# The first mixer's output projection as seven half-size block products, with weight operands prepared beside the recurrence

## The chip, the cores and the metric

The kernel runs on one core of a Trainium2 chip. Five engines work side by side and are ordered by semaphores: TensorE (PE: matmuls, with weight loads shown as PEld), VectorE (DVE), ScalarE (ACT), GpSimd (POOL) and SyncE (SP, which here only issues DMAs). Each engine takes its instructions in the order in which they were written for it. The metric is the device time of one execution in microseconds. Three runs of the kernel before gave 2483.78, 2484.63 and 2484.67 us, a median of 2484.63 us.

## The reference

A trunk of two layers on a 1024 x 1024 activation (1024 tokens, 1024 features), all in float32. The part that the change touches is the first layer's mixer: two branches of 512 features, a spatial gate (`a_out`) and a gated delta rule, a recurrence over the tokens (`b_out`). Both are joined and projected back to 1024 features, and the result is added to the residual `h`, which then goes through a norm into the MLP:

```python
hn = rms_norm(h, ln_mix_e[i])
proj = hn @ w_in_e[i]
a_out = gmlp_spatial_gate(jax.nn.gelu(a_uv), gmlp_v_gain[i], gmlp_ws[i], gmlp_bs[i])
b_out = gated_deltanet(b_qkv, b_z, b_beta, b_a, gdn_conv[i], gdn_a_log[i],
                       gdn_dt_bias[i], gdn_out_gain[i])
h = h + jnp.concatenate([a_out, b_out], axis=-1) @ w_out_e[i]
# every layer goes on with
hn = rms_norm(h, ln_mlp[layer])
h = h + jnp.square(jax.nn.relu(hn @ w_mlp1[layer])) @ w_mlp2[layer]
```

The second layer's mixer is a differential attention, and each layer ends with a gated per-layer embedding. They are not touched.

## The kernel before

**Layout and precision.** The activation is held transposed, features on the 128 partitions: eight feature tiles k or m, and for each two halves of 512 tokens (0 and 1). A matmul takes a 128 x 128 weight block and a 128 x 512 operand. Each float32 operand is split into a rounded part hi and a remainder lo (`split`: a cast on ACT, L315, and a subtraction on DVE, L319), and a product is three matmuls, hi·hi, hi·lo and lo·hi (`mm3`). All matmuls are issued through a helper at L82, so one line number stands for nearly all of them; the tiles' names tell them apart.

**Stages around the change.** `even_mix` runs the first mixer. Its generator `fill` yields after every few matmuls: the input projections (384 steps) and then `mixing()`. The recurrence (`prep` and `step` for chunks 0 to 7) takes its own instructions at a high priority, and between its pieces `pump` takes a number of steps from `fill`; `FILLS` says how many beside each chunk. `Ordered` keeps a filler matmul from being issued more than `LAG` slots ahead of the recurrence. The order of each engine's instructions is made when the program is built, by priority and a simulated time: what is written later can be issued earlier if its inputs and its buffer are free. Tiles of one tag share that tag's slots, so a tile waits for a slot until all who used a former one are done.

**The output projection.** `mixing()` runs `mix_out(0, ...)`, the product for token half 0, as filler. For each output tile m, the weight columns are loaded from `w_out` (into tag raw, 8 slots), split into tag w (12 slots), and multiplied by the eight operand tiles `mixed[0][k]`; the sum goes into the residual tile `acc` (loaded from `h_dram`, added at L1654), whose square is added up for the norm (`add_square`), and the tile is stored to `h_dram` (L1656). `second_gates` is woven in: it makes the gate branch of half 1. After the loop over chunks `put_b(1)` transposes the recurrence's output for half 1, `put_ab` splits it (L1998 and L1999), and `mix_out(1, ...)` runs in `trunk`. Its start issues the norm of half 0: `rms` sums the squares on TensorE, takes the power on POOL (L360), writes the 512 factors to DRAM and reads them back as rows of all partitions (L364, L366, `far=True`), and `norm` scales (L1669), casts (L1675) and subtracts (L1676) each of the eight tiles. `mix_out(1)` also takes five steps of `prepare`, which prepares weights of the second layer from POOL's queue. Then `mlp` begins, first with products of half 0 (`front`), whose weights go through raw and w.

**Seven products elsewhere.** `mlp`, `ple` and `values` already compute 2 x 2 block products with seven half-size products instead of eight (Strassen-Winograd). `prepare_gate` and `ple` do it with weight operands that are summed and split ahead, put into `gate_dram`, and loaded ready.

**Names and lines.** `FILLS`, `prepare_gate` (L249), `split` (L315, L319), `rms` (L349 to L366), `mix_out` (L1613), `put_ab` (L1995), `put_b` (L2002), `mixing` (L2300), `pump` (L2327), the tags raw, w, B, t (four slots), sqs0 and sqs1, and the PSUM tags mm, tr, aux, sc (two banks each).

## Time and profile before

| | us |
|---|---|
| three runs, median | 2484.63 |
| the profiled execution | 2483.4 |
| its span on the core | 2481.7 |
| PE busy | 2468.6 |
| DVE busy | 1856.5 |
| ACT busy | 1352.8 |
| POOL busy | 334.6 |

The profiled execution is one of its own, 1.2 us below the median of the three runs; its span is 1.7 us below its time. A busy engine is one that has an instruction under way; matmuls overlap in a pipeline, so the duration of one is longer than the distance to the next. Rows of groups show busy time and the mean duration in ns, then the idle time before them and what ended it. Rows of DMAs show how many transfers of what size there were and the median us from issue to landing. The recurrence runs from about 206 to 364 us, the output projection from 364 to 463 us, and the first MLP matmul starts at 462.99 us.

### The profile page before, as it was taken

How to read it: one execution, taken by the hardware profiler on the slowest of the kernel's cores; microseconds unless marked ns; L12 is line 12 of the kernel's file. 1: busy time of each engine (PE TensorE's matmuls, PEld its weight loads, DVE VectorE, ACT ScalarE, POOL GpSimd, SP SyncE). 2: the span in 40 equal slices, each digit the busy share in tenths (PEclk: the TensorE clock that was granted, in tenths of full speed). 3: DMA queues.
4: the chain of work that ended last, by engine and by line, in shares of the span. 5: the costliest groups of instructions: out<-in, count | busy, mean ns of one | idle time of the engine just before them, and what ended most of it. 6: DMA issues, size and time to landing. Idle time of an engine off the chain costs nothing.

```text
span 2481.7 us, 39487 instructions
## 1 busy us (share of the span) xinstructions
PE 2468.6 (99%) x13417; PEld 2100.4 (85%) x13417; DVE 1856.5 (75%) x3598; ACT 1352.8 (55%) x2752; POOL 334.6 (13%) x419
## 2 busy tenths in 40 slices
PE   9999999999999999999999999999999999999999
PEld 8898998887888888888889999988788888888887
DVE  7868665788877878777858777776878657788586
ACT  6635473565556445644527777764655554445452
POOL 0211221101111202411112232310000000000000
PEclk9999999999999999999999999999999999999999
DMA  8464435659778957985461311476467458666651
GB/s 240 127 188 108 141 118 186 216 191 320 275 263 312 331 184 239 329 263 189 155 204 52 100 66 58 138 235 210 140 219 249 168 172 307 187 197 196 196 175 64
DMA packets 330131, 478.17 MB, mean 193 GB/s; under 512 B 50276, under 2 KB 161864, under 8 KB 329928
## 3 DMA queue, kind: packets, MB, share of 16 engines
q1 hardware_dynamic: 314136, 426.87, 53.0%
q0 software_dynamic: 15232, 48.25, 5.6%
q8 instruction: 105, 1.72, 0.3%
q14 instruction: 98, 0.80, 0.1%
q10 hardware_dynamic: 560, 0.53, 0.1%
HBM read 327.67 MB, written 147.86 MB: 192 GB/s over the span
## 4 chain that ended last, share of the span: by engine, by line
PE 84%; issue 6%; DMA 4%; DVE 4%; ACT 1%; POOL 1%; SPq 0%; DVEq 0%; POOLq 0%; ACTq 0%
PE mm L82 72%; PE po L82 3%; PE qk L82 2%; PE tr L85 2%; PE aux L82 2%; DMA qk_dram<-w 1%; DVE w L319 1%; DMA gate_dram<-w 1%; DVE g L393 0%; DVE lg L1422 0%; DMA rd<-r 0%; DMA raw<-in_w_mlp_dram 0%; DMA t<-in_p_dram 0%; DMA graw<-gd 0%; ACT w L315 0%
## 5 line engine op out<-in xcount | busy, mean ns | idle before, releaser
L82 PE MATMUL mm<-g,w 128*128 128x512 f32 x2592 | 601.9, 394 | 0.0
L82 PEld LDWEIGHTS mm<-g,w 128*128 128x128 f32 x2592 | 486.7, 188 | 114.1
L315 ACT CAST w<-raw 128x512 fp32r<-128x512 f32 x550 | 335.3, 617 | 405.0 <-PE mm L82 273.3
L82 PE MATMUL mm<-hi,w 128*128 128x512 f32 x1696 | 545.1, 396 | 1.4 <-DVE w L319 1.3
L319 DVE TENSOR_TENSOR w<-raw,w 128x512 fp32r<-128x512 f32 x550 | 372.9, 686 | 173.8 <-ACT w L315 146.1
L82 PE MATMUL mm<-w,hi 128*128 128x256 f32 (+2 forms) x2112 | 438.1, 302 | 0.6 <-DVE k L1332 0.6
L82 PEld LDWEIGHTS mm<-hi,w 128*128 128x128 f32 x1696 | 317.9, 188 | 75.7 <-DVE w L319 2.1
L82 PEld LDWEIGHTS mm<-w,hi 128*128 128x128 f32 x2112 | 338.5, 188 | 17.1 <-DVE k L1332 1.3
L82 PE MATMUL mm<-lo,w 128*128 128x512 f32 x848 | 334.4, 395 | 0.5 <-DVE lo L1676 0.5
L82 PE MATMUL mm<-w,lo 128*128 128x256 f32 (+2 forms) x1056 | 316.0, 300 | 0.0
L82 PE MATMUL mm<-t,w 128*128 128x512 f32 x1152 | 271.3, 394 | 0.5 <-DVE g L393 0.5
L82 PEld LDWEIGHTS mm<-t,w 128*128 128x128 f32 x1152 | 216.4, 188 | 50.9 <-issue 0.9
L82 PEld LDWEIGHTS mm<-w,lo 128*128 128x128 f32 x1056 | 198.8, 188 | 7.9
L82 PEld LDWEIGHTS mm<-lo,w 128*128 128x128 f32 x848 | 159.5, 188 | 35.9 <-DVE lo L1676 1.0
L319 DVE TENSOR_TENSOR g<-graw,g 128x512 fp32r<-128x512 f32 x216 | 147.0, 683 | 4.4 <-DMA gd<-g 1.6
L315 ACT CAST g<-graw 128x512 fp32r<-128x512 f32 x216 | 132.8, 617 | 22.7 <-DMA graw<-gd 10.9
L1425 ACT ACTIVATE lg<-lg,nm 128x128 f32<-128x128 f32 (+7 forms) x128 | 99.3, 776 | 38.6 <-DVE nm L1422 37.5
L360 POOL TENSOR_TENSOR r<-ms,mhalf 128x4 f32<-128x4 f32 x12 | 17.1, 1427 | 739.1 <-DVE ms L358 707.9
L462 ACT ACTIVATE g<-g 128x512 f32<-128x512 f32 x100 | 63.0, 631 | 69.2 <-DVE g L393 69.1
L1422 DVE CUSTOM_DVE_ANT_0 lg<-qk,al 128x512 f32<-128x512 f32 (+3 forms) x128 | 74.2, 586 | 20.3 <-PE qk L82 17.8
L82 PE MATMUL mm<-ohi,w 128*128 128x512 f32 x256 | 83.6, 399 | 0.3 <-DVE acc L1654 0.3
L82 PE MATMUL mm<-ahi,w 128*128 128x512 f32 x256 | 83.1, 400 | 0.3 <-ACT ahi L1998 0.2
(397 smaller groups left out, 3836.4 us busy)
## 6 DMA issues: line engine op xcount, KB each, us to landing
raw<-in_w_mlp_dram SPq DMA_DIRECT2D x352, 256.0 KB, 3.7
graw<-gd SPq DMA_DIRECT2D x224, 256.0 KB, 3.3
gd<-g SPq DMA_DIRECT2D x192, 256.0 KB, 3.6
acc<-h_dram SPq DMA_DIRECT2D x64, 256.0 KB, 4.6
qk_dram<-w POOLq DMA_DIRECT2D x64, 256.0 KB, 5.2
keep<-in_w_mlp_dram SPq DMA_DIRECT2D x64, 256.0 KB, 5.0
w<-qk_dram SPq DMA_DIRECT2D x64, 256.0 KB, 4.2
raw<-in_w_in_e_dram SPq DMA_DIRECT2D x60, 256.0 KB, 3.8
```

Source lines behind the costliest of these rows:

```text
L82: self._next(self.engine.matmul(*a, **k))
L85: self._next(self.engine.transpose(*a, **k))
L315: inst = self.nc.scalar.copy(hi, src)
L319: inst = (lo_engine or self.nc.vector).tensor_tensor(lo, src, f32(hi), ALU.subtract)
L360: nc.gpsimd.tensor_tensor(r, ms, self.mhalf[:, 0:4], ALU.pow)
L462: nc.scalar.activation(g, src, AF.Relu)
L1422: nc.vector.tensor_tensor_reduce(out=lg[:, k0:k1], in0=ps[:, : k1 - k0], in1=al[:, u0 + k0 : u0 + k1], scale=-0.5 ** (hd + 1), scalar=3.0e ...
L1425: nc.scalar.activation(lg[:, :n], lg[:, :n], AF.Exp, bias=nm[:, r, nch - 1 : nch], scale=-1.0, accum_out=me.sums[:, b, r : r + 1])
```

## The change

The weight `w_out` is seen as 2 x 2 blocks of 512 x 512, the operand `mixed` as 2 x 2 blocks (feature half by token half). `prepare_mix` forms, for each of four row tiles k, the seven left operands (four sums or differences and three plain blocks), splits them and stores hi and lo in `mix_dram`; its loads and stores are issued by POOL, the stores of one operand at the start of the next (`late`). Its 29 steps are taken by `pump` on every fourth filler step after step 260. All 28 operands go through one slot, B, of hi and lo; x and y live in the slots sqs0 and sqs1, z in the ring t.

`put_ab` now also forms the right operands: half 0's tiles are stored in `halves`; t1 = half 0 minus half 1 of the gate's features, t2 = half 0 of the recurrence's features minus t1 (also stored), t4 = half 1 of those minus t2. t3, the difference of the two feature halves of token half 0, is formed at the start of `mix_seven`. Half 0 of the gate's features is no longer split itself.

`mix_seven` replaces both `mix_out` calls of the first layer. It runs the products 3, 1, 5, 6, 7 as filler (80 steps), then, after `put_b(1)`, 2 and 4 (32 steps). Each product loads 16 of the 56 x 2 prepared tiles, half of them into tag w, half into tag raw; hi and lo are used straight from there. Four PSUM banks `x` (two of mm, two of tr) hold product 1 and collect 6, 7 and 4 on top of it; the other products go through mm, aux and sc. `add` puts a product into the residual tiles, and with `done` adds the squares and stores. After product 7 half 0 is complete; the norm of half 0 is started inside product 2 and its scaling is written into product 4. Five steps of `prepare` are taken, two before product 4 and three after it. `put_b(1)` gets the high priority. `FILLS` goes from 20, 20, 20, 20, 26, 26, 28, 28 to 18, 18, 18, 18, 24, 26, 30, 30.

```diff
+BEFORE = 260
-FILLS = (20, 20, 20, 20, 26, 26, 28, 28)
+FILLS = (18, 18, 18, 18, 24, 26, 30, 30)
+    def prepare_mix(self, w):
+        nc = self.nc
+        self.mix_dram = self.dp.tile([7, 4, 2, P, HT], F32, name="mix_dram")
+        late = []
+        def put(n, k, src):
+            for out, t in late:
+                nc.gpsimd.dma_start(out, t)
+            late.clear()
+            both = self.slot("B", [P, 2, HT], F32R, "wm")
+            for j, t in enumerate(self.split(src, both[:, 0], both[:, 1])):
+                late.append((self.mix_dram[n - 1, k, j], f32(t)))
+        def get(t, j, l, k):
+            nc.gpsimd.dma_start(t, w[(4 * j + k) * P : (4 * j + k + 1) * P, l * HT : (l + 1) * HT])
+        def tt(out, a, b, op=ALU.subtract):
+            nc.vector.tensor_tensor(out, a, b, op)
+        def pair(k):
+            x, y = (self.sp.tile([P, HT], F32, tag=f"sqs{i}", name=self.nm("wm"), bufs=1) for i in range(2))
+            get(x, 1, 1, k)
+            get(y, 0, 1, k)
+            return x, y
+        x, y = pair(0)
+        yield
+        for k in range(4):
+            put(4, k, x)
+            tt(y, y, x, ALU.add)
+            yield
+            z = self.tmp()
+            get(z, 0, 0, k)
+            put(5, k, y)
+            yield
+            put(1, k, z)
+            tt(y, y, z)
+            yield
+            put(6, k, y)
+            tt(x, x, y)
+            yield
+            put(7, k, x)
+            get(x, 1, 0, k)
+            yield
+            put(2, k, x)
+            tt(x, x, y)
+            yield
+            put(3, k, x)
+            if k < 3:
+                x, y = pair(k + 1)
+            yield
+        for out, t in late:
+            nc.gpsimd.dma_start(out, t)
...
+    def mix_seven(self, h_dram, gain_next, gates, halves, t1s, t2s, side):
+        rings = ("w", WB), ("w", WB), ("raw", RB), ("raw", RB)
...
+        def load(n):
+            a = []
+            for k in R:
+                tag, bufs = rings[k]
+                a.append([self.wp.tile([P, 1, HT], F32R, tag=tag, name=self.nm("w"), bufs=bufs)[:, 0] for _ in range(2)])
+                for j, t in enumerate(a[k]):
+                    nc.sync.dma_start(f32(t), self.mix_dram[n - 1, k, j])
+            return a
...
+        def add(m, h, ps, done=False):
+            t = acc(m, h)
+            nc.vector.tensor_tensor(t, t, ps, ALU.add)
+            if done:
+                self.add_square(h, t)
+                nc.sync.dma_start(h_dram[m, :, h * HT : (h + 1) * HT], t)
+        def third():
+            a[3] = load(3)
+            for q in R:
+                if q == 1:
+                    a[1] = load(1)
+                y = bank("mm")
+                yield from product(q, a[3], self.mixed[0][4:], y, True)
+                add(q, 0, y)
+            a[5] = load(5)
...
+        x = [bank(t) for t in ("mm", "tr", "mm", "tr")]
+        for q in R:
+            yield from product(q, a[1], self.mixed[1][0:4], x[q], True)
+            add(q, 1, x[q])
+        a[6] = load(6)
+        for q in R:
+            y = bank("aux")
+            yield from product(q, a[5], t1s, y, True)
+            add(q, 0, y)
+            add(4 + q, 0, y)
+        a[7] = load(7)
+        for q in R:
+            yield from product(q, a[6], t2s, x[q])
+            add(q, 0, x[q], True)
+        a[2] = load(2)
+        for q in R:
+            yield from product(q, a[7], t3s, x[q])
+            add(4 + q, 0, x[q], True)
+        a[4] = load(4)
+        yield True
+        for q in R:
+            y = bank("sc")
+            yield from product(q, a[2], self.mixed[1][4:], y, True)
+            if q == 0:
+                self.rb[0] = self.rms(0, self.sqs[0], far=True)[1]
+            add(q, 1, y, True)
+        next(side, None)
+        next(side, None)
+        for q in R:
+            yield from product(q, a[4], t4s, x[q])
+            if q == 0:
...
+                    inst = nc.vector.scalar_tensor_tensor(t, t, gain_next[:, m : m + 1], self.rb[0], ALU.mult, ALU.mult)
...
+            add(4 + q, 1, x[q], True)
+        for _ in range(3):
+            next(side, None)
...
         def put_ab(hf, k, pt):
...
+            if not hf:
+                t = self.tmp()
+                nc.scalar.copy(t, flat(pt))
+                nc.sync.dma_start(halves[k], t)
+            if hf or k > 3:
+                self.mixed[hf][k] = self.split(flat(pt), *self.hs_parts(hf, k))
+            if hf and k < 4:
+                u, v = self.tmp(), self.tmp()
+                nc.sync.dma_start(u, halves[k])
+                nc.vector.tensor_tensor(u, u, flat(pt), ALU.subtract)
+                t1s.append(self.split(u, *self.hs_parts(1, 4 + k)))
+                nc.sync.dma_start(v, halves[4 + k])
+                nc.vector.tensor_tensor(v, v, u, ALU.subtract)
+                t2s.append(self.split(v, *self.hs_parts(0, 4 + k)))
+                nc.sync.dma_start(t2_dram[k], v)
+            elif hf:
+                u = self.tmp()
+                nc.sync.dma_start(u, t2_dram[k - 4])
+                nc.vector.tensor_tensor(u, flat(pt), u, ALU.subtract)
+                self.t4s.append(self.split(u, *self.hs_parts(1, k - 4)))
...
         def mixing():
+            for _ in parts:
+                pass
             self.new_hs()
+            seven.append(self.mix_seven(h_dram, gain_next, second_gates(), halves, t1s, t2s, side))
+            yield from iter(lambda: next(seven[0]), True)
...
+                if done > BEFORE and done % 4 == 0:
+                    next(parts, None)
...
-        for _ in put_b(1):
+        with self.tc.high_priority(EARLY):
+            for _ in put_b(1):
+                pass
+        for _ in seven[0]:
             pass
```

77 lines of the change are left out of this document (55 added, 22 removed).

## The prediction

> **What bounds the kernel now.** I read the page's busy shares and its chain of waits first, then the busy time of the stages around the change, then the pitch of the matmuls inside the chain.
>
> ```profile
> PE 2468.6 (99%) x13417; PEld 2100.4 (85%) x13417; DVE 1856.5 (75%) x3598; ACT 1352.8 (55%) x2752; POOL 334.6 (13%) x419
> PE 84%; issue 6%; DMA 4%; DVE 4%; ACT 1%; POOL 1%; SPq 0%; DVEq 0%; POOLq 0%; ACTq 0%
> 206.00:364.00 158.00, 158.00 (x1277) 151.19 (x1275) 105.74 (x246) 85.60 (x235) 38.19 (x31) 1.00 0.40 118
> 364.00:463.00 99.00, 98.74 (x468) 80.56 (x468) 65.02 (x122) 46.63 (x88) 15.40 (x23) 1.00 0.65 208
> L82 PE MATMUL mm<-ahi,w 128*128 128x512 f32 x256 | 83.1, 400 | 0.3 <-ACT ahi L1998 0.2
> L82 PE MATMUL mm<-alo,w 128*128 128x512 f32 x128 | 50.5, 394 | 0.0
> 780.61 254.28 PE mm L82 x1097
> 661.21 66.90 PE mm L82 x288
> ```
>
> The third and fourth rows are stages; after the times stand the busy us of PE, PEld, DVE, ACT and POOL, the granted clock, the DMA share and GB/s. From 206 to 364 us run the eight recurrence chunks with the input projections as filler; from 364 to 463 us run all 256 + 128 = 384 matmuls of the output projection, with gates between them. TensorE is busy in all of both stages, and 84% of the chain is its own. So a matmul taken out is worth its pitch, unless something else becomes late. The 394 and 400 ns are overlapped durations; the pitch is 254.28/1097 = 0.232 us, and 66.90/288 = 0.232 us again.
>
> **What goes.** The direct product is 8 x 8 blocks x 2 halves x 3 matmuls = 384, as the rows count. Seven products of 4 x 4 blocks x 3 make 336. 48 fewer x 0.232 = 11.1 us, nothing added on TensorE: transposes, gate matmuls and the norm's sums stay. One product is 48 matmuls, again 11.1 us. The changed filler shares move work between chunks and cost nothing on an engine without gaps.
>
> **What comes on the other engines.** Operand preparation beside the recurrence: 28 casts, 28 remainders, 16 sums, 16 loads and 56 stores from POOL. Prices:
>
> ```profile
> L315 ACT CAST w<-raw 128x512 fp32r<-128x512 f32 x550 | 335.3, 617 | 405.0 <-PE mm L82 273.3
> L319 DVE TENSOR_TENSOR w<-raw,w 128x512 fp32r<-128x512 f32 x550 | 372.9, 686 | 173.8 <-ACT w L315 146.1
> L246 POOL DMA_DIRECT2D qk_dram<-w x64: 540/557/602, 432.6 to 1087.5; - x64
> L244 POOL DMA_DIRECT2D raw<-in_w_qkv_o_dram x10: 702/722/928, 404.7 to 446.8; - x10
> ```
>
> DVE 44 x 0.686 = 30.2, ACT 28 x 0.617 = 17.3, POOL 56 x 0.557 + 16 x 0.722 = 42.7 us. Added to the 158 us stage: DVE 136, ACT 103, POOL 81. All fit, so I cost their throughput at nothing; the cover is the stage's idle time (52 us of DVE). In the projection's stage DVE loses 32 weight remainders and gains 12 (28 right operands instead of 16), 16 differences and 16 more block additions: +12 x 0.686 = 8 us, 73 of some 90 us. ACT loses 32 casts and gains 12, and 8 copies. Nothing there either. What can be late are three waits.
>
> **First wait: the put chain on one buffer.** Each of the 28 puts casts into the same slot (tag B), so a cast waits until both stores of the put before have landed. The POOL stores cost, over the run and in two 20 us windows (after POOL busy again clock, DMA share, GB/s):
>
> ```profile
> qk_dram<-w POOLq DMA_DIRECT2D x64, 256.0 KB, 5.2
> gate_dram<-w POOLq DMA_DIRECT2D x56, 256.0 KB, 3.8
> 680.00:700.00 20.00, 20.00 (x88) 16.22 (x87) 13.81 (x23) 11.48 (x21) 3.23 (x6) 1.00 0.85 281
> gate_dram<-w POOLq DMA_DIRECT2D x4, 256.0 KB, 3.4
> 580.00:600.00 20.00, 19.41 (x84) 15.35 (x82) 17.32 (x29) 11.58 (x20) 2.16 (x4) 1.00 0.94 340
> gate_dram<-w POOLq DMA_DIRECT2D x4, 256.0 KB, 5.0
> L82 PEld LDWEIGHTS pz<-yt,work x64: 129/135/135, 206.3 to 208.1; 64*64 64x64 f32 x64
> w<-gate_dram SPq DMA_DIRECT2D x56, 256.0 KB, 5.3
> ```
>
> The narrow windows' stores are the row just below each. The slot's former content (yt) is last read at 208.1 + 0.1 = 208.2 us, so with a landing of L the puts are over at 208.2 + 28 x (0.617 + 0.686 + L), and the operand is back in SBUF 5.3 us later. The third product comes first and needs the last put. It is due where the first projection matmul starts now, at 364 us, plus six units that need only blocks 0 to 2 (6 x 0.696 = 4.2; two PSUM banks allow no more): 368 us. That holds for L up to 4.2. The stage moves 118 GB/s; 72 transfers of 0.262 MB over 158 us add 119, together 237, a share of about 0.8. That is nearest the window at 0.85, where L is 3.4: ready at 345 us, no loss. With 5.0, from the window at 0.94, it is ready at 390, a loss of 22 us. I take 0 and keep both ends.
>
> The Trainium skill ("DMA: Bandwidth & Descriptors", section on the anatomy of a POOL-issued DMA) fits such a transfer as 2.0 us plus bytes over 436 GB/s, 2.6 us for 256 KB. By it the chain would be over 22 us earlier still, and this wait could not decide; the rows just shown are slower than the fit at every load, so I go by them.
>
> **Second wait: the DMA engines.** Between 364 us and the end of the fifth product SP has to bring some 94 tiles of 0.262 MB: 46 operand tiles, 16 residual tiles, 8 + 8 + 4 halves and t2 tiles, 4 for the gate; and 4 + 4 are stored. That is 24.6 MB in 80 units x 0.696 = 55.7 us plus the 9.9 us that the stage holds beside its 384 matmuls (99 - 384 x 0.232), 375 GB/s. The 340 GB/s window above lost 0.6 us of TensorE; this one none:
>
> ```profile
> 780.00:800.00 20.00, 20.00 (x89) 16.36 (x90) 15.49 (x25) 11.23 (x21) 0.00 (x0) 1.00 1.01 376
> ```
>
> At 376 the loss is 0, at 340 it is 24.6/0.340 - 65.6 = 6.8 us. I take 0: the 376 window, too, is mostly SP loads of prepared tiles for running matmuls. 6.8 stays as the other end.
>
> **Third wait: the norm in front of the MLP.** Now the first half's norm is started with 39.8 us of matmuls still ahead of the MLP (423.24 to 462.99):
>
> ```profile
> 423.24 0.95 PE L82 MATMUL aux<-ones,sqs 128*128 128x1 f32 x8
> 427.44 0.38 SPq L364 DMA_DIRECT2D rd<-r  x1
> 436.72 0.34 SPq L366 DMA_DIRECT2D rb<-rd  x1
> DMA to landing us min/median/max: 4.4/5.3/9.3
> 441.76 1.42 DVE L1669 SCALAR_TENSOR_TENSOR acc<-acc,cols,rb 128x512 f32<-128x512 f32 x2 [1.06 <-DMA rb<-rd]
> 452.30 0.69 DVE L1676 TENSOR_TENSOR lo<-acc,hi 128x512 fp32r<-128x512 f32 x1
> 462.71 0.69 DVE L1676 TENSOR_TENSOR lo<-acc,hi 128x512 fp32r<-128x512 f32 x1
> 462.99 0.39 PE L82 MATMUL mm<-hi,w 128*128 128x512 f32 x1
> L319 DVE TENSOR_TENSOR w<-raw,w 128x512 fp32r<-128x512 f32 x11 | 7.4, 686 | 0.0
> L1669 DVE SCALAR_TENSOR_TENSOR acc<-acc,cols,rb 128x512 f32<-128x512 f32 x8 | 5.9, 748 | 1.1 <-DMA rb<-rd 1.1
> L1676 DVE TENSOR_TENSOR lo<-acc,hi 128x512 fp32r<-128x512 f32 x8 | 5.5, 688 | 0.0
> L342 DVE TENSOR_TENSOR sqs<-sqs,t 128x512 f32<-128x512 f32 x4 | 2.7, 686 | 0.0
> L1654 DVE TENSOR_TENSOR acc<-acc,mm 128x512 f32<-128x512 f32 x4 | 2.7, 682 | 0.0
> ```
>
> After the change half 0 is complete only when the seventh product ends (call it tau); only the second and fourth follow: 2 x 11.1 = 22.3 us. The sum of squares is ready at about tau + 2.0 (add 0.686, square about the same, add), its matmul stands behind the second product's first quarter, tau + 2.8. From that matmul to the first scaling it now takes 441.76 - 423.24 = 18.5 us, of which 9.3 are the write of r (landings of that pair: 4.4, 5.3, 9.3 at minimum, median, maximum). While that lasts SP's issue of rb waits and everything behind it on SP with it: residual and MLP loads.
>
> With the median of 5.3 the scaling starts at tau + 17.3. Its eight tiles took 21.6 us here (441.76 to 463.40), the first four 11.2 (to 452.99), in a stretch where DVE had no gap: 35 instructions, the counts of the five last rows. Of these some 27 are left (16 of the norm, 4 adds and squares of the fourth product, 7 remainders for MLP and qk weights), so 16.7 and 8.7 us. The MLP's first product wants its fourth tile 9 matmuls in, at tau + 24.4, and gets it at 26.0: 1.6 us. The next wants the eighth at 22.3 + 1.6 + 33 x 0.232 = tau + 31.6 and gets it at 34.0: 2.4. Together 4.0 us, which I take. Lower end: landing 4.4, DVE for the norm alone (0.748 + 0.688 a tile): the fourth tile at tau + 22.8 and the eighth at 28.5, no wait. Upper end: landing 9.3 and today's spacing: the fourth at 32.5 (8.1 late), the eighth at 42.9 against 38.1, in all 12.9.
>
> The MLP's weights wait as well, because operands now sit in the raw ring (8 slots) until their matmuls are through:
>
> ```profile
> raw<-in_w_mlp_dram SPq DMA_DIRECT2D x352, 256.0 KB, 3.7
> raw<-in_w_qkv_o_dram POOLq DMA_DIRECT2D x64, 128.0 KB, 5.3
> ```
>
> At tau + 11.1 the second product gives up four; the five qk raws come first, split by 11.1 + 5.3 + 1.3 = 17.7, then MLP raws land at 21.4 and are split at 22.7, hidden in the 1.6 us. If they must wait for the fourth product's slots instead: 22.3 + 3.7 + 1.3 = 27.3, 5.0 us late, inside the 12.9.
>
> **Sum.** The profiled execution took 2483.4 us: 2483.4 - 11.1 + 0 + 0 + 4.0 = 2476.3. The median of the runs shown, 2484.63, is 1.2 above it, so 2477.5 for the median, 0.29% faster.
>
> **Rivals.**
>
> *The DMA engines bound the stage.* For: 375 GB/s asked, and the 340 row with its 0.6 us. Against: the 376 row. Price 6.8 us: 2484.3, no change. Also here: a late landing that eats 3 to 9 us anywhere in that stage.
>
> *Slower: the put chain is late.* Place: the single slot B, and the third product's last block. It decides from L = 4.2 us on; from 4.45 on the whole gain is gone (28 x 0.25 = 7 us). At L = 5.0 it is 2477.5 + 22 = 2500. For: the 5.2 median, and casts that already wait in order on ACT for such stores:
>
> ```profile
> ACT w L315 <- DMA qk_dram<-w: 28.2, 10, 7.7
> ACT w L315 <- DMA gate_dram<-w: 26.0, 13, 5.5
> ```
>
> (us in total, times, longest.) A cast so blocked holds up the recurrence's copies behind it on ACT. Against: the 3.4 at a share of 0.85.
>
> *The norm costs its full price:* 2484.63 - 11.1 + 12.9 = 2486.4. For: 9.3 us was the landing at this very place. Against: the instructions that leave DVE.
>
> **Chances.** About 0.2% (5 us) is what a measurement of this kernel can tell from no change: faster means below 2479.7, slower above 2489.6. My forecast, 2473.5 to 2481: 0.46 (0.43 faster, 0.03 same). DMA: 0.24 (0.04, 0.16, 0.04 slower). Put chain: 0.22 (0.03 same, 0.19 slower). Full norm: 0.08 (0.04, 0.04). Sums: 0.47, 0.26, 0.27. The likeliest case alone spans 2473.5 to 2481; the range runs from 2473 (nothing lost: 2473.5) to 2496, a put chain with L up to about 4.85, and leaves out its worst part.
>
> **What would show it.** Right: 336 matmuls in the projection's stage at 0.232 us; TensorE without gaps up to tau; one gap of a few us just before the first MLP matmuls, released by DVE's lo or w. Wrong: a gap before the third product's last block with ACT waiting on the prepared stores (put chain); gaps released by loads of prepared operands with the DMA share at 1.0 (DMA bound); ACT or DVE near full from 206 to 364 us with the recurrence's matmuls waiting for them, which would void the costing at nothing.

## Result and profile after

The changed kernel takes 2574.35 us (median of four runs, 2570.62 to 2580.56) against 2484.25 us for the kernel before on the same chip: a ratio of 1.0365, 95% interval 1.0342 to 1.0389. It is 90 us slower where 7 us faster was forecast, and outside the range of 2473 to 2496.

The page of the changed kernel (the profiled execution took 2580.56 us, 6 above the median): its span, the busy shares, TensorE and its granted clock in 40 slices, the chain of waits, and the group that holds most of the projection's matmuls.

```profile
span 2578.8 us, 39762 instructions
PE 2482.0 (96%) x13369; PEld 2105.7 (82%) x13369; DVE 1888.3 (73%) x3654; ACT 1362.3 (53%) x2768; POOL 378.2 (15%) x491
...
PE   9999984869999999999999999999999999999999
...
PEclk9999996979999999999999999999999999999999
...
PE 83%; DMA 5%; DVE 5%; issue 4%; ACT 1%; POOL 1%; SPq 0%; DVEq 0%; POOLq 0%; ACTq 0%
...
L83 PE MATMUL mm<-hi,w 128*128 128x512 f32 x1920 | 626.8, 401 | 58.2 <-ACT w L371 25.7
```

The 48 matmuls are gone (13417 to 13369), but TensorE now idles 2578.8 - 2482.0 = 96.8 us where it idled 13.1, and is busy 13.4 us longer with 11.1 us less work, 24.5 us more than its work at the old pitch. Most of these 24.5 us are matmuls at a lower granted clock: TensorE's busy time times what the clock lacks to 1.00, added up over windows of 1 us, comes to 22.5 us (0.0 in the kernel before). The idle time grew by 83.7 us, and 83.7 + 13.4 = 97.1 us, the whole difference of the spans. The damage is in slices six to nine, 322 to 580 us. Which waits these are (who waited, for whom, then total us, times and longest; `guv` and `pgm` belong to the gate branch, `pab` is a transposed block in PSUM that `put_ab` takes over):

```profile
PE mm L83 <- ACT w L371: 25.7, 1, 25.7
PE mm L83 <- DVE t L2177: 11.8, 2, 9.6
PE mm L83 <- DMA w<-mix_dram: 9.3, 2, 5.7
PE mm L83 <- issue: 8.3, 1, 8.3
PE pgm L83 <- DVE guv L2138: 7.0, 1, 7.0
PE pgm L83 <- ACT t L2170: 6.0, 3, 3.9
```

They stand at three places. **First, inside the five products**, from 370 to 443 us. Four of the 10 us windows (busy us of PE, PEld, DVE, ACT, POOL, granted clock, DMA share, GB/s):

```profile
370.00:380.00 10.00, 4.92 (x26) 4.06 (x25) 3.14 (x13) 5.98 (x18) 8.51 (x9) 0.74 0.93 337
...
390.00:400.00 10.00, 2.92 (x6) 1.70 (x6) 2.68 (x5) 1.24 (x2) 1.08 (x2) 0.60 0.96 328
...
420.00:430.00 10.00, 3.98 (x10) 2.54 (x10) 4.33 (x7) 1.82 (x3) 1.44 (x3) 0.50 0.93 270
430.00:440.00 10.00, 2.90 (x6) 1.82 (x6) 3.96 (x6) 1.76 (x3) 2.16 (x4) 0.51 0.46 163
```

No engine is full there; the window from 430 has not even a busy DMA. The prepared operands' transfers (the view of one tile: count, shortest/median/longest issue in ns, first and last start; then what the issuing engine waited for, and who waited for the transfers) say why. The last row is of the DMA view, with the median us from issue to landing of the 56 stores:

```profile
L1690 SPq DMA_DIRECT2D w<-mix_dram x56: 319/381/1188, 335.9 to 492.1; - x56
L307 POOL DMA_DIRECT2D mix_dram<-wm x54: 539/539/637, 211.0 to 433.0; - x54
L352 POOL DMA_DIRECT2D mix_dram<-wm x2: 539/540/542, 437.7 to 438.5; - x2
...
  ACT wm L371: 102.1, 25
...
  ACT wm L371: 49.4, 13
...
mix_dram<-wm POOLq DMA_DIRECT2D x56, 256.0 KB, 3.5
```

(The 56 loads are eight tiles for each of the seven products, out of 28 x 2 prepared ones; the section on the change says 16 of 56 x 2, which is wrong.) The stores were to be over at 340 us, and the last operand back in SBUF at 345; the last store is issued at 438.5. All through the products the preparation still runs, and its casts stand in ACT's order between the products' own. The timeline, all engines:

```profile
376.58 0.62 ACT L371 CAST wm<-wm 128x512 fp32r<-128x512 f32 x1 [3.51 <-DMA mix_dram<-wm]
377.11 0.58 ACT L2170 COPY t<-pab 128x512 f32<-128x512 f32 x1
...
377.74 1.22 PE L83 MATMUL pgm<-guv,wT 128*128 128x128 f32 x4 [3.90 <-ACT t L2170]
...
430.42 0.62 ACT L371 CAST wm<-wm 128x512 fp32r<-128x512 f32 x1 [6.10 <-DMA mix_dram<-wm]
...
436.27 0.62 ACT L371 CAST hi<-t 128x512 fp32r<-128x512 f32 x1 [5.23 <-DVE t L2177]
436.38 0.77 PE L83 MATMUL mm<-hi,w 128*128 128x512 f32 x1 [9.56 <-DVE t L2177]
436.79 0.61 ACT L371 CAST wm<-wm 128x512 fp32r<-128x512 f32 x1
...
442.81 0.52 PE L83 MATMUL mm<-hi,w 128*128 128x512 f32 x1 [3.53 <-DMA w<-mix_dram]
```

At 376.58 a cast of the preparation has waited 3.5 us for the former store out of slot B; the copy of a transposed block stands behind it on ACT, and TensorE waits 3.9 us for that copy. At 430.42 such a cast waits 6.1 us, and the last one follows at 436.79; between them stands a cast of the products' own, which waits 5.2 us for a half that is read back from DRAM. The last prepared block is then stored (437.7 and 438.5) and loaded again, and the third product gets it at 442.81. By then 42 of the 240 matmuls of the five products have run; the others follow without a gap to the end of the seventh product at 491.4 us, 62 us behind the 429.6 that were reckoned. **Second**, 8.3 us ahead of the second product, and **third**, 25.7 us ahead of the MLP (rows of the timelines; SPq is SP's queue of DMA issues):

```profile
492.56 3.48 SPq L2185 DMA_DIRECT2D t<-t_dram  x4
...
498.87 1.32 DVE L2186 TENSOR_TENSOR t<-pab,t 128x512 f32<-128x512 f32 x2 [5.33 <-DMA t<-t_dram]
...
499.67 0.77 PE L83 MATMUL mm<-hi,w 128*128 128x512 f32 x1 [8.29 <-issue]
...
518.75 15.08 SPq L1706 DMA_DIRECT2D h_dram<-acc  x5
...
522.75 1.42 DVE L1768 SCALAR_TENSOR_TENSOR acc<-acc,cols,rb 128x512 f32<-128x512 f32 x2 [11.01 <-DMA rb<-rd]
...
533.92 2.16 SPq L497 DMA_DIRECT2D raw<-in_w_mlp_dram  x4
...
549.69 0.20 ACT L1331 ACTIVATE lame<-lame 128x2 f32<-128x2 f32 x1 [8.81 <-DVE lame L1330]
...
551.02 0.79 PE L83 MATMUL mm<-hi,w 128*128 128x512 f32 x1 [25.69 <-ACT w L371]
```

t2 is read back only at 492.56, after the seventh product, and until it lands the pab tiles, by the code, hold the PSUM banks of the second product. The norm's chain starts late with it: the first scaling is at 522.75. SP, in order, then holds five stores of h, each waiting for its tile, for 15 us; the MLP's first weights are asked for only at 533.92; and ACT, in order, waits 8.8 us in the attention's constants before it may cast them. The MLP starts at 551.0 us; it was 463.0.

### The profile page after: what moved, and what is told of

Same layout as the page of the kernel before. It is cut to its first block, busy times and chain, and to the rows that moved or that the text cites. A ratio compares the mean times of both kernels' runs of the same rounds, so it can differ in the third digit from the quotient of the medians.

```text
span 2578.8 us, 39762 instructions
## 1 busy us (share of the span) xinstructions
PE 2482.0 (96%) x13369; PEld 2105.7 (82%) x13369; DVE 1888.3 (73%) x3654; ACT 1362.3 (53%) x2768; POOL 378.2 (15%) x491
## 4 chain that ended last, share of the span: by engine, by line
PE 83%; DMA 5%; DVE 5%; issue 4%; ACT 1%; POOL 1%; SPq 0%; DVEq 0%; POOLq 0%; ACTq 0%
PE mm L83 72%; PE po L83 3%; PE qk L83 2%; PE tr L86 2%; PE aux L83 2%; DMA raw<-in_w_mlp_dram 1%; DVE w L375 1%; DMA mix_dram<-wm 1%; DVE raw L449 1%; DMA uv_dram<-t 1%; DMA gate_dram<-w 0%; DMA gd<-g 0%; DVE g L449 0%; DVE lg L1478 0%; DMA t<-halves 0%
## 5 line engine op out<-in xcount | busy, mean ns | idle before, releaser
L83 PE MATMUL mm<-hi,w 128*128 128x512 f32 x1920 | 626.8, 401 | 58.2 <-ACT w L371 25.7
L371 ACT CAST w<-raw 128x512 fp32r<-128x512 f32 x518 | 315.2, 617 | 373.1 <-PE mm L83 258.8
L83 PEld LDWEIGHTS mm<-hi,w 128*128 128x128 f32 x1920 | 365.4, 191 | 146.8 <-ACT w L371 26.1
L375 DVE TENSOR_TENSOR w<-raw,w 128x512 fp32r<-128x512 f32 x518 | 350.0, 684 | 163.1 <-ACT w L371 126.9
L83 PE MATMUL mm<-lo,w 128*128 128x512 f32 x960 | 383.9, 400 | 1.7 <-DVE lo L375 1.0
L83 PEld LDWEIGHTS mm<-lo,w 128*128 128x128 f32 x960 | 183.6, 191 | 44.1 <-DVE lo L375 2.2
L518 ACT ACTIVATE g<-g 128x512 f32<-128x512 f32 x100 | 63.0, 631 | 74.6 <-DVE g L449 74.3
L519 ACT ACTIVATE g<-g 128x512 f32<-128x512 f32 x128 | 80.5, 631 | 2.2
```

The costliest lines, as they stand in the source:

```text
L83: self._next(self.engine.matmul(*a, **k))
L371: inst = self.nc.scalar.copy(hi, src)
L375: inst = (lo_engine or self.nc.vector).tensor_tensor(lo, src, f32(hi), ALU.subtract)
L518: nc.scalar.activation(g, src, AF.Relu)
L519: nc.scalar.activation(g, g, AF.Square)
```

## Experiments

All times are medians; ratios are to the kernel before on the same chip, whose medians lay between 2484.25 and 2486.65 us. The points in us are read off TensorE's timeline of the one profiled execution of each kernel, which lies up to 7 us from its median: differences of a few us between such points, or between a point and a median, tell little. The prediction had the first product at 364.0, the end of the seventh at 429.6 and the MLP at 453.5 (463.0 - 11.1 + 1.6). "One operand prepared" and "half the loads" leave parts of the work out.

| kernel | first product | end of seventh | gap, then second product | gap ahead of MLP | time | ratio (95%) |
|---|---|---|---|---|---|---|
| changed | 378.6 | 491.4 | 8.3 | 25.7 | 2574.35 | 1.0365 (1.0342-1.0389) |
| raw ring | 382.3 | 465.1 | 7.3 | 25.0 | 2547.18 | 1.0257 (1.0239-1.0275) |
| one operand prepared | 365.5 | 442.9 | 6.9 | 23.8 | 2523.13 | 1.0160 (1.0144-1.0176) |
| constants late | 378.5 | 488.2 | 7.2 | 18.2 | 2565.26 | 1.0326 (1.0309-1.0342) |
| norm without DRAM | 381.5 | 492.6 | 7.3 | 6.1 | 2561.97 | 1.0311 (1.0294-1.0327) |
| raw ring, early | 414.7 | 494.4 | 7.9 | 25.5 | 2575.50 | 1.0358 (1.0341-1.0376) |
| the same, four orders | 414.5 | 491.6 | 7.7 | 6.5 | 2560.73 | 1.0300 (1.0285-1.0315) |
| half the loads | 365.7 | 441.0 | 9.9 | under 1 | 2499.20 | 1.0061 (1.0044-1.0077) |
| raw ring, z in B | 375.3 | 452.4 | 7.4 | 24.5 | 2537.49 | 1.0211 (1.0195-1.0226) |
| combined | 371.6 | 448.0 | 7.3 | 6.1 | 2514.56 | 1.0119 (1.0104-1.0134) |
| raw slots alone | 377.8 | 489.0 | 8.3 | under 2 | 2560.25 | 1.0305 (1.0290-1.0321) |
| all repairs | 374.2 | 448.8 | 9.2 | under 1 | 2518.27 | 1.0139 (1.0122-1.0156) |
| t2 earlier | 373.1 | no gap | none | 10.3 | 2506.92 | 1.0081 (1.0059-1.0104) |
| t2 earlier, raw slots | 371.5 | no gap | none | under 1 | 2507.76 | 1.0080 (1.0053-1.0106) |

### The slot B

```diff
-            both = self.slot("B", [P, 2, HT], F32R, "wm")
-            for j, t in enumerate(self.split(src, both[:, 0], both[:, 1])):
+            both = [self.wp.tile([P, 1, HT], F32R, tag="raw", name=self.nm("wm"), bufs=RB)[:, 0] for _ in range(2)]
+            for j, t in enumerate(self.split(src, *both)):
```

> The 28 puts take hi and lo from the raw ring (8 slots) instead of the one slot B; nothing else changes. If the put chain on B is what makes the third product late, the casts stop waiting for the stores of the put before, the puts end near 365 us instead of 438, the third product does not wait, the seventh ends near 430 instead of 491 us, and the time falls by about 60 us to 2515 (2500 to 2530). Rival: the ring t (where z lies) or the in-order queues of ACT and POOL set the pace of the puts, not the slot. Then they still end after 420 us and the time stays within 10 us of 2574.

27 us came back, not 60: the time lies between the two ranges, and the seventh product ends at 465.1. The stores now have eight slots and still end only at 390. A second holder appears in POOL's timeline: between the first two rows it issued no transfer of the preparation. By the code z waits there for a slot of the ring t; the run with z in B, below, tests it.

```profile
207.72 0.54 POOL L307 DMA_DIRECT2D mix_dram<-wm  x1 [2.66 <-DVE wm L375]
...
240.26 0.61 POOL L314 DMA_DIRECT2D t<-in_w_out_e_dram  x1
248.03 0.54 POOL L307 DMA_DIRECT2D mix_dram<-wm  x1 [7.16 <-ACT wm L371]
```

### No preparation to wait for

```diff
+        both = self.slot("B", [P, 2, HT], F32R, "wm")
+        parts = self.split(x, both[:, 0], both[:, 1])
         for k in range(4):
-            put(4, k, x)
...
+            for n in (4, 5, 1, 6, 7, 2, 3):
+                for j, t in enumerate(parts):
+                    nc.gpsimd.dma_start(self.mix_dram[n - 1, k, j], f32(t))
+                yield
```

> Leaves out 27 of the 28 operand preparations: one block is loaded, split once, and its two parts are stored 56 times to the places of all operands (so the projection's result is another one). The store traffic and the loads of the products stay; the chain, its casts, remainders and sums go. If the chain is the cause: about as the kernel with the raw ring, 2515 (2500 to 2530), and any lower time is what the preparation's engine work cost. Rival: the DMA engines bound the stage (375 GB/s asked). Then the seventh product still ends 20 us or more after 430 us, and the time is 2535 or more.

51 us below the changed kernel. The DMA rival fell. The products start where they were reckoned to (365.5), so the late start elsewhere is the preparation, not the filler's new shares. But the seventh product still ends 13 us late, and the two later gaps are untouched: some 38 us of the loss are not the preparation.

### The attention's constants behind the MLP

```diff
-        T.attn_consts(attn_q_gain[0], attn_k_gain[0], diff_lambda[0], attn_sub_gain[0], lam_init)
...
+            T.attn_consts(attn_q_gain[0], attn_k_gain[0], diff_lambda[0], attn_sub_gain[0], lam_init)
             T.ple(pT, acc, w_ple_proj[0]
```

> The constants of the attention (among them the exponentials of diff_lambda, loaded by SP and computed on ACT) are written behind the first layer's MLP instead of before it; all else as in the changed kernel. If ACT's wait for that load (8.8 us before the first MLP weights are cast) is on the path, the MLP starts about 9 us earlier and the time is about 2565. Rival: the MLP's weights, whose loads were issued late, would have ended at the same point: within 4 us of 2574.

As expected: 9.1 us less, and the gap ahead of the MLP went from 25.7 to 18.2 us.

### The norm without the way through DRAM

```diff
-                self.rb[0] = self.rms(0, self.sqs[0], far=True)[1]
+                self.rb[0] = self.rms(0, self.sqs[0])[1]
```

Without `far` the factors are spread over the partitions by four matmuls of the code (eight rows: 13377 instead of 13369) instead of a store and a read; where later expectations speak of the norm's place in TensorE's order, it is this edit.

> The norm of half 0 spreads its factors with four transposing matmuls and a copy instead of through DRAM; all else as in the changed kernel. If the trip through DRAM (rd, rb) is what starts the norm late, the scaling starts some 13 us earlier, SP is not held for rd's landing, the MLP starts 13 to 20 us earlier: 2555 to 2561. Rival: the MLP's weights or ACT's wait for diff_lambda come last anyway: less than 5 us gained, 2569 or more.

12.4 us less, just short of the 13 expected; the gap ahead of the MLP fell to 6.1 us, with another of 3.3 us for a weight behind it.

### An earlier preparation, and four orders behind the products

```diff
-BEFORE = 260
+BEFORE = 100
```

The second kernel adds the two edits just shown and lets POOL issue the reads of t2 and the stores of `add`:

```diff
-                nc.sync.dma_start(u, t2_dram[k - 4])
+                nc.gpsimd.dma_start(u, t2_dram[k - 4])
...
-                nc.sync.dma_start(h_dram[m, :, h * HT : (h + 1) * HT], t)
+                nc.gpsimd.dma_start(h_dram[m, :, h * HT : (h + 1) * HT], t)
```

> The raw-ring kernel of the first experiment (2547.2 us) with its preparation begun 160 steps of the recurrence's filling earlier (from step 100 instead of 260). Nothing is left out. Theory A, the pace of the chain: what still delayed the products there was that the last stores ended at 388 to 390 us, 20 us after the products should begin; with an earlier start they end before 368 us, the queue is empty when the products' loads begin, and the time falls to that of the kernel with one operand prepared, about 2523 us (2515 to 2530), with the end of the seventh product at about 440 us. Rival B, the DMA engines are the bound from 380 us on whenever the stores are made, because the 28 pairs of loads (14.7 MB with the rest of the stage) must pass anyway: the time stays at 2540 to 2550 us. Rival C, the operands' loads and casts share the raw ring with the recurrence's projections and delay those: a gap appears before 340 us and the time is above 2550 us.

> The kernel of the run beside it (raw ring, early start) with four edits of order behind the products: the constants of the second layer's attention read after the first MLP instead of ahead of it; half 0's norm sums placed at their place in TensorE's order instead of far behind; the four reads of t2 and the eight last stores of h issued by POOL instead of SP. Nothing is left out. Theory: the tail of 25 us was made of these waits, one after the other: the constants are worth 9 (as measured alone), the norm 12 (as measured alone), the second gap of 8 about 7, the stores ahead of the MLP's loads 5; together about 30 us, at most the 33 of the two gaps: 2490 us (2483 to 2503) if the run beside it is at 2523, and in any case 25 to 33 us below it. Rival: the tail is bound by the weights and the scalings themselves, not by these orders; then the two edits already measured do not add, and it is only 12 to 15 us below the run beside it.

Theory A fell, rival C held. The stores end at 227 us, and the loss only moved: the first product starts 50 us late. Two rows of the timeline and one of the windows, all of the early kernel:

```profile
159.80 1.44 PE L83 MATMUL mm<-w,hi 128*128 128x256 f32 x5 [12.59 <-ACT w L371]
...
232.74 3.46 PE L83 MATMUL py<-dt,ay 32*32 32x32 f32 x122 [15.67 <-DVE dt L2326]
```

```profile
220.00:240.00 20.00, 7.26 (x138) 6.44 (x139) 15.61 (x33) 9.38 (x16) 3.19 (x6) 0.51 0.67 210
```

The first is a projection's matmul that waits for the cast of its weight, and the projections' weights come through the raw ring. The second is a matmul of the recurrence behind a chain of steps on DVE; with the projections held back TensorE had nothing to do beside it. From the first product to the end of the seventh it takes 79.7 us, hardly more than with one operand prepared (77.4): what was expected of the products held, what was expected of the stage ahead did not. The four orders bring 15 us instead of 25 to 33, as the rival said (12 to 15): the constants and the norm do not add, since they end at the same matmul, and the reads of t2 from POOL brought nothing (the gap ahead of the second product stayed at 7.7 us). What the stores from POOL did by themselves was not measured.

### Half the loads

```diff
-                a.append([... for _ in range(2)])
-                for j, t in enumerate(a[k]):
-                    nc.sync.dma_start(f32(t), self.mix_dram[n - 1, k, j])
+                t = self.wp.tile([P, 1, HT], F32R, tag=tag, name=self.nm("w"), bufs=bufs)[:, 0]
+                nc.sync.dma_start(f32(t), self.mix_dram[n - 1, k, 0])
+                a.append([t, t])
```

> The kernel with one operand prepared (2523.1 us) that also loads only the first of each operand's two parts and uses it for both: 28 loads of 256 KB instead of 56, everything else as there. Left out: 27 of the 28 prepared operands, and the second part of every prepared operand in the three matmuls of a product. There the end of the seventh product stood at 442.9 us, 13 us behind the 429.6 that were expected, with the DMA engines at 0.96 to 1.03 of their time. Theory A, the bytes are what is left of the lateness: with 7.3 MB less, the end of the seventh product comes to 430 to 434 us and the time to about 2511 us (2507 to 2516). Rival B, it is the gates' and the pab tiles' chain of small steps between the products, which no byte touches: the time stays within 2520 to 2526 us.

Neither range was met. Theory A fell on its own point: the seventh product ends at 441.0 instead of 442.9, so in a kernel without the preparation the bytes of the operands are not what delays the products. The time still fell by 24 us, at another place that neither theory had named: the gap ahead of the MLP is gone. The timeline shows both:

```profile
378.67 2.05 SPq L2109 DMA_DIRECT2D guv<-uv_dram  x1
...
387.21 2.16 DVE L2120 SCALAR_TENSOR_TENSOR guv<-pgm,cols,guv 128x128 f32<-128x128 f32 x8 [0.60 <-DMA guv<-uv_dram]
...
388.39 1.86 PE L83 MATMUL pgm<-guv,wT 128*128 128x128 f32 x7 [5.01 <-DVE guv L2120]
...
441.06 0.38 SPq L479 DMA_DIRECT2D raw<-in_w_mlp_dram  x1
```

Here u is half 1's part of the gate branch, stored to DRAM by the projections. Half 1's gate waits for its read, and with it, by the code, the transposes and the first and fifth products' operands; only the third product is there to cover it. And with half as many tiles in the raw ring, the MLP's weights were asked for from 441 us, at the end of the seventh product, instead of 482 with one operand prepared.

### z in the free slot B, and the repairs combined

```diff
-            z = self.tmp()
+            z = self.slot("B", [P, HT], F32, "wm")
```

> The raw-ring kernel of the first experiment (2547.2 us), in which the quarter z is read into the slot B, which the raw ring has left free, and not into the ring t. Nothing is left out. Theory A: there the first z waited for a slot of ring t in order of program (its read was issued at 240.3 us, 33 us behind the second pair's stores, and the last z's cast was at 363.5 us); without these waits the stores follow at the pace of the steps and end before 365 us, the products are delayed only by their own loads, and the time falls to about that of the kernel with one operand prepared, 2525 us (2518 to 2532). Rival B: the stores are issued by POOL in order between its work of the recurrence, and this sets the pace, not z: the last store stays after 375 us and the time at 2538 to 2550 us.

> The kernel of the run beside it (raw ring, z in B) with a step of the preparation after every third step of the filling instead of every fourth, the attention's constants read after the first MLP, and half 0's norm sums at their place in TensorE's order. Nothing is left out. Theory: the two edits behind the products are worth what they were alone, 9 and 12 us, and the faster pace 0 to 5 us: 21 to 26 us below the run beside it, 2502 us (2494 to 2511) if that is at 2525; it does not reach the 2484 us of before, because the products' own loads (some 13 us) and the waits of the two gaps that are left (7 and 6 us) exceed what the 48 matmuls save (11 us). Rival: with the stores out of the way the tail edits and the pace together reach 2484 us or less.

z was the second holder: the last stores come at 334 us instead of 390, and the seventh product ends 12.7 us earlier, at 452.4. So theory A's mechanism held; its time did not, since the median fell by only 9.7 us, to just below rival B's range. The two profiled executions differ by 12.7 us, as the points do, but the one here is the fastest of its four runs. The combined kernel is 22.9 us below it, inside the 21 to 26 expected of it, but at 2514.6 us.

### The raw slots alone, and with everything

```diff
-                tag, bufs = rings[k]
+                tag, bufs = rings[0 if n == 2 else k]
```

with the five `next(side, None)` of `mix_seven` left to the MLP; the second kernel is the combined one with these two edits and

```diff
-            y = bank("sc")
+            y = bank("aux")
             yield from product(q, a[2], self.mixed[1][4:], y, True)
```

> The changed kernel with two edits for the raw ring alone: the second product's operands lie wholly in the ring w, so that four of the eight raw slots are free when the seventh product ends, and the five steps that prepare the second layer's weights between the products (they load into raw slots) are made in the MLP. Nothing is left out. Theory A: the last gap (25.7 us ahead of the MLP's first matmul) ends with a cast of a weight because the MLP's first weights get slots and a place in SP's order only behind the products; in the run with half of each operand loaded the raw ring had free slots, its MLP started 34 us behind the end of the seventh product instead of 56, and that gap was gone. Here the gap falls to what the norm needs, at most 12 us, and the time by 12 to 22 us, to 2552 to 2563 us. Rival B: the gap is the norm's and the constants' alone, as the two runs that moved these (12 and 9 us) would have it; the time stays at 2568 to 2580 us.

> All repairs together: raw ring and z in B, a step after every third step of the filling, the attention's constants behind the first MLP, the norm's sums at their place, the two raw-ring edits of the run beside it, and the second product's sums in the banks aux instead of the bank that the pab tiles hold. Nothing is left out. Theory: against the run without the last three edits (2514.6 us) the gap of 7.3 us ahead of the second product and the one of 6.1 us ahead of the MLP close for the most part, 9 to 13 us: 2503 us (2500 to 2507), still above the 2484 us of before, since the products' own stage stays some 12 us longer than its matmuls. Rival: the bank and the slots open an order that also lets the MLP's own products run without waits; then 2490 us or less.

Theory A held: with the norm and the constants as they were, the 25.7 us gap is gone, the largest wait near it being this one, and 14.1 us are won by the medians (the profiled executions, the fastest of this kernel and the slowest of the changed one, differ by 23.3).

```profile
525.51 0.73 PE L83 MATMUL mm<-hi,w 128*128 128x512 f32 x2 [1.68 <-DVE w L375]
```

With all repairs the expectation was missed by 15 us: the gap ahead of the second product stayed (9.2 us, now released by the cast of t4's hi, behind the same read of t2; the pab tiles hold the aux banks as well as sc). The gap of 6.1 us ahead of the MLP is gone, and waits of 1.4, 2.5, 0.7 and 0.7 us appear at 864 to 888 us instead. Whether the three edits help stays open: its four runs spread over 9 us around those of the combined kernel.

### The reads of t2 earlier, u from POOL

```diff
         a[7] = load(7)
+        yield True
         for q in R:
             yield from product(q, a[6], t2s, x[q])
...
         a[4] = load(4)
-        yield True
...
-            nc.sync.dma_start(gu[:, :, 0:h1], uv_dram[0, ...])
+            (nc.gpsimd if hf else nc.sync).dma_start(gu[:, :, 0:h1], uv_dram[0, ...])
```

> The kernel of the run with raw ring, z in B, steps after every third, constants late and norm sums near (2514.6 us) with two edits of order: the reads of t2 and the fourth product's operands are written in the code ahead of the sixth product instead of behind the seventh, and the gate's read of u for the second half is issued by POOL instead of SP. Nothing is left out. Theory A: the gap of 7.3 us ahead of the second product is the read of t2 (landing some 5 us behind an issue that comes only when the seventh product's squares give up the slots of ring t), while the pab tiles hold the banks; written earlier it is gone. The gap of 5.7 us ahead of the second half's gate matmuls is the read of u behind halves and residual tiles in SP's order; issued by POOL, idle there, it is 2 us or less. Together 9 to 12 us with what the slower clock behind the gaps adds: 2503 us (2500 to 2507). Rival B: the banks or the transposes' own turn hold the second product, or the landing rather than the issue of u sets the gate; then a gap of the same size stays at that place and the time is above 2509 us.

> The kernel of the run beside it with the two raw-ring edits (second product's operands wholly in the ring w; the five steps of the next weights' preparation made in the MLP). Nothing is left out. Theory: the 6 us ahead of the MLP go, but in the run with all repairs these two edits cost about as much again inside the MLP (gaps of 1 to 2.5 us at its casts): 2500 us (2495 to 2505), above the 2484 us of before by the late start of the products, the stage's own waits and the norm's chain that two products do not cover. Rival: with the gaps closed the clock stays full and the saved 48 matmuls show: below 2490 us.

The time, 2506.92 us, is just inside theory A's range. The first edit did what A said: TensorE has no gap from 420 to 470 us, and the second product follows at once; the gap ahead of the MLP grew from 6.1 to 10.3 us. Windows of that kernel:

```profile
430.00:440.00 10.00, 10.00 (x45) 8.09 (x45) 6.17 (x11) 3.01 (x5) 0.00 (x0) 1.00 0.98 320
440.00:450.00 10.00, 10.00 (x49) 8.23 (x48) 10.00 (x17) 5.80 (x11) 0.00 (x0) 1.00 0.84 300
```

The second edit did what B said of the gate: a gap of the same size stays. From its timeline:

```profile
386.61 0.85 POOL L2127 DMA_DIRECT2D guv<-uv_dram  x1 [11.84 <-DMA uv_dram<-t]
...
395.44 3.69 PE L83 MATMUL pgm<-guv,wT 128*128 128x128 f32 x16 [5.64 <-DVE guv L2138]
```

POOL, idle there, waited for u itself to land in DRAM. The gate's gap is the store and the read one after the other, not SP's queue. The last kernel closes the gap ahead of the MLP too and is no faster (2507.76 against 2506.92, ranges overlapping); 2495 to 2505 was expected. Its page:

```profile
PE 2468.4 (99%) x13377; PEld 2097.5 (84%) x13377; DVE 1890.0 (75%) x3654; ACT 1361.0 (54%) x2769; POOL 380.3 (15%) x492
```

Of its span of 2505.7 us TensorE idles 37.3 against 13.1 before: by windows of 50 us, 5.4 more from 200 to 350 us (recurrence, with the preparation beside it), 9.6 from 350 to 450 (the products), 8.7 around 850 to 900 and 1100 to 1150 us in the MLP. And it is as busy as before (2468.6) with 11.1 us less to do: by the sum over windows of 1 us the lower granted clock takes some 6 us of that, the norm's added matmuls about 1, and the rest is not accounted for. So no version tried beats the kernel before: the saved 11 us do not come out of TensorE's busy time, and 24 us more are idle.

## Why the prediction was wrong

**The saving** (48 x 0.232 = 11.1 us): the count was right, and in undisturbed stretches the pitch is as before. What failed is the assumption that a matmul costs its pitch in either kernel: behind the long gaps it costs more. TensorE is busy 24.5 us beyond its work, 22.5 of them by the granted clock.

**Throughput at nothing:** right as far as it went. ACT is at 53%, DVE at 73%. The cost came through the order on these engines.

**The first wait, the put chain: the step that failed.** The mechanism was named as a rival, with the place where it would show, and its sign is there: a gap before the third product's last block at 442.81, with casts on ACT that wait for the stores. The landing was taken rightly: 3.4 us against a measured median of 3.5 (2.9 up to 280 us, 3.3 up to 368, 4.9 from there to 440), so that by the prediction's own bound of 4.2 no loss was due. The formula around it was wrong. It gave 0.617 + 0.686 + 3.4 = 4.7 us a put. Measured from cast to cast, the third put (the first z, cast at 247.35 us) came 31 us behind the second; from there to the twenty-first at 376.58 the 18 intervals are 7.2 us on average, and the seven after it 8.6. Missing, by the trace, were the stores' deferral to the next step, their two issues one after the other (0.54 each), POOL's own work of the recurrence between them, ACT's order, and z, which by the description of the change lies in the ring t and which the prediction put at nothing. The slot and z were tested: giving the puts the raw ring won 26.3 us at the end of the seventh product, and z in B another 12.7. With both gone the deferral and POOL's work are still there, and the puts follow each other at 4.9 us (first stores from 199.8 to 333.0 us, 27 intervals): these things cost what they cost through the one slot and through z. The combined kernel, with a step after every third and the two edits behind the products, ends it 4.4 earlier still, and with one operand prepared it ends 5.1 before that (448.0 to 442.9): 48.5 of the 61.8 us. How the last 9.5 us divide between these two steps is not firm, since three edits lie between the kernels. The prediction also let a late chain delay one block only. In fact 198 of the five products' 240 matmuls ran only after that block, a blocked cast held what stood behind it on ACT (the 3.9 us at 377.74), and the rival priced at 22 us cost more than twice that.

**The second wait, the DMA engines:** the 0 that was taken stands, against the rival, as far as it was tested: with one operand prepared, halving the operands' bytes moved the end of the seventh product by 1.9 us, though the DMA share there had been 1.01 and 1.03 from 380 to 400 us. Of the 11.4 us that remain (441.0 - 429.6) TensorE is idle for 8.2, and 5.5 of these are waits for half 1's gate. That wait was not in the list: the store and the read of u, formerly covered by an output projection that could run without it. No run took it away. The rest is small waits, a first product 1.7 us late and some 1.4 us of lower clock.

**The third wait, the norm ahead of the MLP,** taken at 4.0 us with 12.9 as the upper end, measured 551.0 - 491.4 - 22.3 = 37.3 us for all that is lost there. The sentence that failed is that the wait of the MLP's weights for raw slots is "hidden in the 1.6 us", at most 5.0: freeing the slots alone closes a gap of 25.7 us. The estimate counted slots and saw that the write of r would hold SP, but not the five stores of h, each waiting for its tile, that stand ahead of these loads. The norm itself was late as well: with the end of the seventh product as tau, its sums run at tau + 14.3 us (505.71) and not at 2.8, behind the gap ahead of the second product and its slow clock, and the first scaling is at tau + 31.4 and not at 17.3. The write of r took 10.3 us of that (508.01 to 518.34), beyond the upper end. Not listed at all were the constants ahead of the MLP on ACT and the read of t2 (8.3 us), for which the fourth product's operands hold PSUM banks. The waits overlap: 9 and 12 us one by one, 14 for the slots, and each alone leaves another.

**After the MLP's start** the spans differ by another 9.1 us (2578.8 - 551.0 against 2481.7 - 463.0), which was not foreseen; gaps over 0.3 us there sum to 11.7 instead of 6.6, and the lower clock, by the sum over windows of 1 us, is worth another 4.1. Which order causes these gaps was not tried.

## What to carry over

A chain through one buffer is priced by its whole cycle, with the deferral, the issues and everything that stands between them in the order of each engine, not by the work and the landing; and what a blocked instruction holds up behind it is a price of its own. When a long product that covers latencies is cut into seven short ones, list every round trip through DRAM that it covered (here u, t2, r, the next weights) and ask which of the short ones still covers each. A gap that closes when you move one wait may be held by three; only the kernel without all of them shows what the order is worth.

## What the hardware showed

The price of a gap is more than the gap. Windows of 2 us of the changed kernel behind the 8.3 us gap:

```profile
499.00:501.00 2.00, 1.33 (x3) 1.16 (x4) 1.95 (x4) 1.24 (x2) 0.00 (x0) 0.50 0.22 80
501.00:503.00 2.00, 2.00 (x6) 1.52 (x5) 2.00 (x4) 0.84 (x2) 0.00 (x0) 0.50 0.00 0
503.00:505.00 2.00, 2.00 (x6) 1.54 (x6) 1.05 (x3) 0.40 (x1) 0.00 (x0) 0.60 0.00 0
505.00:507.00 2.00, 2.00 (x14) 1.81 (x13) 0.83 (x2) 0.63 (x1) 0.06 (x1) 1.00 0.24 90
```

The granted clock is 0.50 from the first matmul at 499.67 us on, 0.60 in the window from 503 and 1.00 in the last. Meanwhile a matmul follows the last at 0.43 us instead of 0.232: eleven of them take the 4.83 us to 504.50, where 2.55 would do, so the gap costs some 2.3 us on top of itself. The Trainium skill ("TensorE: Matmul & The Clock Gate", Part 1: The HAM clock gate) has the array at half rate after an idle window of about 3.4 us and back after as long a busy one; the trace agrees in kind, with about 5 us until full speed here. Such stretches make up 22.5 of the 24.5 us by which TensorE is busy beyond its work.
